# GpSimd's work outside the mixers moves to VectorE, and a tile's seven products run through three PSUM banks

## The chip, the cores and the metric

The kernel runs on one core of a Trainium2 chip. The metric is device time in microseconds (us). Three runs of the kernel before took 2840.35, 2843.02 and 2845.91 us; the median is 2843.02 us. A core has five engines that the profile names PE (TensorE, matmuls; its weight loads are PEld), DVE (VectorE), ACT (ScalarE), POOL (GpSimd) and SP (SyncE, which issues the loads). Each runs its own list of instructions in order and waits by semaphores for the others.

## The reference

Two layers of a hybrid backbone work on 512 latent tokens and 256 context tokens of width 1024. Each layer has a feed-forward part, a mixer (attention and others) and a second feed-forward part. The change touches the feed-forward parts and the vectors that modulate their inputs:

```python
def rms_norm(x, g):
    x32 = x.astype(jnp.float32)
    y = x32 * lax.rsqrt(jnp.mean(x32 * x32, axis=-1, keepdims=True) + EPS)
    return (y * g.astype(jnp.float32)).astype(x.dtype)

def modulate(h, shift, scale):
    return h * (1 + scale) + shift

def swiglu(h, w_gu, w_down):
    gate, up = jnp.split(h @ w_gu, 2, axis=-1)
    return (jax.nn.silu(gate) * up) @ w_down

def macaron_ffn(x, g, shift, scale, gate, w_gu, w_down):
    h = modulate(rms_norm(x, g), shift, scale)
    return x + 0.5 * gate * swiglu(h, w_gu, w_down)
```

Shift, scale and gate are products of a 1024 by 9216 matrix per layer with silu(c) for the latent tokens (vector 0 in the kernel) and with silu(c_ctx) for the context tokens (vector 1). The inner width of the feed-forward part is 2816, that is 22 tiles of 128.

## The kernel before

The activations stay in SBUF, features on partitions, tokens along the free axis. Every fp32 operand of a matmul is split in two parts: ACT casts the high part (`fill`, L324), DVE subtracts it from the source for the low part (L325), and each product is three matmuls (`mm3`, L303 to L305).

There are four feed-forward sub-layers. The text calls them FFN00, FFN01, FFN10 and FFN11 (layer, first or second). The first three work on 768 tokens, FFN11 on the 512 latent tokens. FFN00 runs to about 600 us of the profiled execution, FFN01 from about 1160 to 1640, FFN10 from about 1765 to 2200, FFN11 from about 2490 to the end; the mixers lie between.

In a feed-forward sub-layer the first three tiles (in FFN00 five) are plain products. The other tiles, 17 in FFN00 and 19 in each other sub-layer, are made by `gu_w`. It treats gate and up as a 2 by 2 block product and takes Winograd's seven block products in place of eight. Each of the seven is 12 matmuls (4 k tiles, three matmuls each) on half of the tokens: 384 columns, in FFN11 256. For that, sums of weight blocks are needed in each tile (POOL, L516, L517, L519, L522) and sums of input blocks once per sub-layer (`combos`: T1 and T2 on DVE, T3 and part of T4 on POOL, L486 to L488, L508, L509; cast and low part L481, L482). The seven products go to five PSUM banks. ACT copies two of them out (L541, L544), DVE adds the others in SBUF (L547 to L560), and the result is split (`finish`, L414, L415). After two to four tiles, a chunk, `down` multiplies them by the second matrix and DVE adds the result to the residual (L316).

FFN00 and FFN01 also carry jobs: `mod_jobs` works out the modulation vectors of later sub-layers from rows of weights, 128 rows by 512 features in a job. For vector 0 DVE multiplies and sums in one instruction (L153; a short one reads the sum out). For vector 1 POOL multiplies (L149) and ACT sums (L150). At the start of the program (`start_up`) the same is done with rows of 1024 for the first norm, tile by tile, between the first products, and POOL makes the low part of one of three weight tiles (L325). POOL also adds up the squares of all later norms (L239).

The order on each engine is set by a scheduler that works with modelled costs. `issue_after` fixes an instruction's turn behind another: products stand behind the last product (`pe_last`), jobs behind the last DVE step of a tile (`dve_last`), and the vector 1 multiply behind the last of the combos on POOL (`pool_last`). Raw weights have two buffers (`wraw`), split weight blocks six slots while there are jobs and eight otherwise, rows of the jobs two (`NWM`).

Of the kernel before, what the change touches and what calls it, by code (L numbers as in the profile page):

```python
# [15 lines left out]
ALU = mybir.AluOpType  # L16
# [37 lines left out]
def hybrid_backbone_kernel(ctx: ExitStack, tc: tile.TileContext, A: dict, out: bass.AP):  # L54
# [9 lines left out]
    def opened(name, **kw):  # L64
        """a pool that is open from here until its second part is called"""
        es = ExitStack()
        return es.enter_context(tc.tile_pool(name=name, bufs=1, reuse_waits="tile", **kw)), es.close

    # PSUM: four banks, and four more that are single or in pairs as the phase wants them
# [20 lines left out]
    # ---------------------------------------------------------------- constants  # L90
# [13 lines left out]
    def load_constants(pool, l, shape):  # L104
        """per-head gains (those of the queries with the scores' factor, negated), head selectors and their transposes"""
# [14 lines left out]
    # ---------------------------------------------------------------- work that is emitted between groups of products  # L120
    pending = []
    down_last, act_last, pool_last = [], [], []
# [13 lines left out]
    # ---------------------------------------------------------------- adaLN vectors  # L136
    def load_silc(tiles, d0, n):
        """silu(c) and silu(c_ctx), n elements from d0, on every partition"""
        for v, t in enumerate(tiles):
            nc.sync.dma_start(t, A["cb"][:, v, d0:d0 + n])  # L140
            ACT.activation(t, t, AF.Silu)
        return tiles

    def mod_row(w, junk, silc, vecs, outs, behind=()):
        """products of 128 rows of weights with silc, an element of the vector per partition"""
        for v in vecs:
            if v == 1:
                with issue_after(pool_last):
                    POOL.tensor_tensor(w, w, silc[v], op=ALU.mult)  # L149
                ACT.activation(w, w, AF.Copy, accum_out=outs[v])  # L150
                continue
            with issue_after(behind):
                V.tensor_tensor_reduce(junk, w, silc[v], 1.0, 0.0, ALU.mult, ALU.add, outs[v])  # L153
# [16 lines left out]
    def mod_jobs(items):  # L170
        """items: (layer, sub, kind, vecs); a job takes 128 elements' products with a half of the features"""
# [23 lines left out]
    # ---------------------------------------------------------------- root mean square, inverse  # L195
# [4 lines left out]
    def rsqrt_sqrt(y, v, pool, shape, tag):  # L200
        """y = v ** -0.5; y and v: [p, n]: root, reciprocal and a Newton step"""
# [8 lines left out]
    def rsqrt_newton(y, v, pool, shape, tag):  # L210
        """the same, v normal and above 0, without the root: a first guess by exponent, then three Newton steps"""
# [7 lines left out]
    class Norm:  # L219
        """RMSNorm and modulation of columns [c0, c0+n) of x into hh, hl"""  # L220

        def __init__(self, c0, n, l, s, eng=POOL, room=None, tail=0):
            self.tail = tail
            self.c0, self.n, self.l, self.s, self.eng = c0, n, l, s, eng
# [3 lines left out]
        def add(self, kt):  # L228
# [4 lines left out]
            else:  # L233
# [5 lines left out]
                self.eng.tensor_tensor(self.acc[:, :self.n], self.acc[:, :self.n], sq[:, :self.n], op=ALU.add)  # L239

        def sums(self):
# [9 lines left out]
            (rsqrt_newton if self.eng is V else rsqrt_sqrt)(y[:, :nt], ms[:, :nt], sm, [P, nt], "rt")  # L251
# [29 lines left out]
    # ---------------------------------------------------------------- weight blocks, split in two float32r parts  # L281
    def wsplit(pool, r, bufs, tag="w", eng=V):
        """[128, n] -> two float32r parts, n at most 1024"""
# [7 lines left out]
    def wload(src, n=2048, parts=2):  # L291
        """one load of two blocks"""
# [4 lines left out]
    def by_k(w, k=KT):  # L297
        """split block [128, k * c] -> one (high, low) pair per k tile"""
# [8 lines left out]
    def issue_after(ins):  # L307
        """what is traced inside takes its turn on the engine behind ins"""
# [9 lines left out]
    # ---------------------------------------------------------------- half-step SwiGLU  # L318
    def fill(w, src, eng=V, behind=()):
        """a float32 block -> its two float32r parts"""  # L320
# [9 lines left out]
    def lead_ffn(fi):  # L330
        """the weights of the first three tiles, a part at a time; then where they are, and how to let go of them"""
# [10 lines left out]
    def lead_mixer(src, name):  # L342
        """the first blocks of an input projection, likewise"""
# [15 lines left out]
    def ffn(l, f, with_ctx, jobs=(), next_sub=None, opening=False, lead_in=None, lead_out=None):  # L359
        """Gate and up products of a tile are a 2 by 2 block product (gate / up, halves of the features,  # L360
        halves of the tokens). The first tiles take it as it stands, while the norms and the sums of blocks
        are being finished; the others take Winograd's seven block products."""
# [10 lines left out]
        with tc.tile_pool(name=f"ffn{fi}", bufs=1, reuse_waits="tile") as fp:  # L373
# [10 lines left out]
            def lead_slots():  # L384
                """[128, 512] pairs for the weights of the first three tiles, a pair per two k tiles"""
# [20 lines left out]
            def lead_k(w):  # L406
                """per k tile: gate and up"""
# [9 lines left out]
            def activate(act, c0, g, u):  # L417
                """of one stream's gate and up"""
# [10 lines left out]
            def gate_up(n):  # L429
                """places for a gate and an up product of n columns"""  # L430
# [22 lines left out]
            def lead(ws, each=None):  # L453
                """first tiles, k outermost, one stream after the other, while the norms are being finished"""
# [20 lines left out]
            def combos():  # L475
                """sums of blocks of the input: T1, T2, T3 and -T4"""
# [17 lines left out]
                for k in range(4):  # L494
# [5 lines left out]
                    sums(POOL, b, b22, b12)  # L500
                    done(2, k, b)
                for k in range(4):
# [5 lines left out]
                    POOL.tensor_tensor(a, b21[0], b, op=ALU.subtract)  # L508
                    pool_last[:] = [POOL.tensor_tensor(a, a, b21[1], op=ALU.add)]  # L509
                    dve_last[:] = [done(3, k, a)]  # L510

            def gu_w(ft):
# [3 lines left out]
                POOL.tensor_tensor(f3, a11, a21, op=ALU.subtract)  # L516
                POOL.tensor_tensor(a21, a21, a22, op=ALU.add)  # L517
                s1 = put(a21)
                POOL.tensor_tensor(a11, a21, a11, op=ALU.subtract)  # L519
                s2 = put(a11)  # L520
                w12 = put(a12)
                POOL.tensor_tensor(a12, a12, a11, op=ALU.subtract)  # L522
                s4 = put(a12)
                s3 = put(f3)
# [12 lines left out]
                oa, oc, ob, od, oe = (bank()[:, :nh] for _ in range(5))  # L537
                sg = sg_tile()
                product(oa, w11, hh[:, TOP, H1], hl[:, TOP, H1])
                x1 = tmp("t2")  # L540
                ACT.copy(x1, oa)  # L541
                product(oc, s1, *tblk[0])
                x5 = tmp("t2")
                ACT.copy(x5, oc)  # L544
                product(ob, s2, *tblk[1])
                u2 = tmp("nacc")
                dve_last[:] = [V.tensor_tensor(u2, ob, x1, op=ALU.add)]  # L547
                product(oa, w12, hh[:, BOT, H1], hl[:, BOT, H1], first=False)
                ACT.activation(sg[:, H1], oa, AF.Silu)
# [3 lines left out]
                product(od, s3, *tblk[2])  # L553
                dve_last[:] = [V.tensor_tensor(u2, od, u2, op=ALU.add)]
                V.tensor_tensor(x5, x5, u2, op=ALU.add)
# [3 lines left out]
                product(oe, w22, *tblk[3])  # L559
                V.tensor_tensor(u2, oe, u2, op=ALU.add)  # L560
                V.tensor_tensor(sg[:, H1], sg[:, H1], u2, op=ALU.mult)
# [91 lines left out]
    def start_up(tiles, slots, lead_k, fill, lead):  # L653
        """loads, first adaLN vectors, first norm and first tiles of the first sub-layer, k by k"""
# [6 lines left out]
        nl = Norm(*LAT, 0, 0, V)  # L661
        nctx = Norm(*CT, 0, 0, V)
# [868 lines left out]
```

## Time and profile before

| | |
|---|---|
| median of 3 runs | 2843.02 us |
| span of the profiled execution | 2841.2 us |
| time around the span, to the median | 1.8 us |
| PE busy | 2648.6 us (93%) |
| DVE busy | 2188.0 us (77%) |
| ACT busy | 1213.8 us (43%) |
| POOL busy | 978.1 us (34%), 677 instructions |
| chain that ended last | PE 62%, DVE 18%, ACT 4%, POOL 2% |

The profile's page gives busy time and the granted clock of TensorE as shares of full speed; a clock of 1.00 is 2.4 GHz throughout, and a lower one is a mean over stretches at 2.4 and at 1.2 GHz. Busy time of an engine counts overlapping instructions once, so the durations in a list of instructions add up to somewhat more. Where a row ends in square brackets, the engine stood idle for that many us before the instruction, and the name behind the arrow is what ended the wait.

### The profile page before, as it was taken

How to read it: one execution, taken by the hardware profiler on the slowest of the kernel's cores; microseconds unless marked ns; L12 is line 12 of the kernel's file. 1: busy time of each engine (PE TensorE's matmuls, PEld its weight loads, DVE VectorE, ACT ScalarE, POOL GpSimd, SP SyncE). 2: the span in 40 equal slices, each digit the busy share in tenths (PEclk: the TensorE clock that was granted, in tenths of full speed). 3: DMA queues.
4: the chain of work that ended last, by engine and by line, in shares of the span. 5: the costliest groups of instructions: out<-in, count | busy, mean ns of one | idle time of the engine just before them, and what ended most of it. 6: DMA issues, size and time to landing. Idle time of an engine off the chain costs nothing.

```text
span 2841.2 us, 42081 instructions
## 1 busy us (share of the span) xinstructions
PE 2648.6 (93%) x15826; PEld 2393.1 (84%) x15826; DVE 2188.0 (77%) x3820; ACT 1213.8 (43%) x2512; POOL 978.1 (34%) x677
## 2 busy tenths in 40 slices
PE   3699999999999999899999988999999989999999
PEld 2589888987977788799899877999998767988988
DVE  8979889986466844998899877777777577577877
ACT  5334444444344542344444443333334455444443
POOL 4555545542121111555455323222212010143432
PEclk9899999999999999999999999999999999999999
DMA  6323333333111241133333321333323200303232
GB/s 236 106 75 117 123 110 123 112 114 117 63 55 48 67 158 38 49 123 113 121 112 108 99 83 53 107 104 108 115 97 104 81 31 1 119 35 108 93 108 90
DMA packets 81172, 271.69 MB, mean 96 GB/s; under 512 B 11002, under 2 KB 15518, under 8 KB 66248
## 3 DMA queue, kind: packets, MB, share of 16 engines
q1 hardware_dynamic: 80408, 268.76, 27.7%
q8 instruction: 124, 2.03, 0.3%
q14 instruction: 80, 0.66, 0.1%
q0 software_dynamic: 560, 0.24, 0.0%
HBM read 262.35 MB, written 5.24 MB: 94 GB/s over the span
## 4 chain that ended last, share of the span: by engine, by line
PE 62%; DVE 18%; ACT 4%; issue 3%; DMA 3%; POOL 2%; SPq 0%; DVEq 0%; ACTq 0%; POOLq 0%
PE ps L303 9%; PE ps L304 9%; PE ps L305 9%; PE pb L303 7%; PE pb L304 7%; PE pb L305 7%; DVE wl L325 5%; DVE junk L153 2%; PE pp L303 2%; PE pp L304 2%; PE pp L305 2%; PE ps L767 2%; ACT wh L324 2%; DVE xn L316 1%; DMA wm<-in_wmod 1%
## 5 line engine op out<-in xcount | busy, mean ns | idle before, releaser
L324 ACT CAST wh<-wr 128x512 fp32r<-128x512 f32 (+1 forms) x672 | 385.9, 590 | 571.6 <-PE pb L304 177.3
L325 DVE TENSOR_TENSOR wl<-wr,wh 128x512 fp32r<-128x512 f32 (+1 forms) x672 | 554.4, 837 | 93.7 <-ACT wh L324 88.8
L149 POOL TENSOR_TENSOR wm<-wm,silc 128x512 f32<-128x512 f32 x176 | 266.5, 1514 | 297.6 <-DVE mod L153 100.9
L303 PE MATMUL ps<-hh,wh 128*128 128x384 f32 (+2 forms) x728 | 252.1, 347 | 24.0 <-ACT u L541 18.9
L305 PE MATMUL ps<-hh,wl 128*128 128x384 f32 (+2 forms) x728 | 250.6, 344 | 2.2 <-DVE wl L325 1.2
L304 PE MATMUL ps<-hl,wh 128*128 128x384 f32 (+2 forms) x728 | 250.4, 344 | 0.0
L153 DVE CUSTOM_DVE_ANT_0 junk<-wm,silc 128x512 bf16<-128x512 f32 x240 | 225.2, 938 | 25.2 <-DMA wm<-in_wmod 20.1
L516 POOL TENSOR_TENSOR s<-wr 128x512 f32<-128x512 f32 x74 | 112.1, 1515 | 378.1 <-DMA wr<-in_wgs 245.8
L303 PE MATMUL pb<-hh,wh 128*128 128x384 f32 (+2 forms) x632 | 210.3, 333 | 29.6 <-ACT u L541 18.3
L304 PE MATMUL pb<-hl,wh 128*128 128x384 f32 (+2 forms) x632 | 209.4, 332 | 26.5 <-DVE hl L269 26.5
L303 PE MATMUL ps<-ah,wh 128*128 128x512 f32 (+1 forms) x640 | 218.9, 348 | 4.5 <-DVE u L560 3.7
L304 PE MATMUL ps<-al,wh 128*128 128x512 f32 (+1 forms) x640 | 220.7, 345 | 0.4 <-DVE al L415 0.4
L305 PE MATMUL ps<-ah,wl 128*128 128x512 f32 (+1 forms) x640 | 219.8, 344 | 0.0
L305 PE MATMUL pb<-hh,wl 128*128 128x384 f32 (+2 forms) x632 | 208.4, 330 | 0.2 <-DVE wl L325 0.2
L303 PE MATMUL pb<-tt,wh 128*128 128x384 f32 (+2 forms) x600 | 195.7, 326 | 13.5 <-ACT tt L481 13.5
L303 PE MATMUL pb<-ah,wh 128*128 128x512 f32 (+1 forms) x576 | 197.9, 354 | 7.6 <-DVE u L560 3.8
L304 PE MATMUL pb<-al,wh 128*128 128x512 f32 (+1 forms) x576 | 202.3, 351 | 2.5 <-DVE al L415 1.4
L304 PE MATMUL pb<-tt,wh 128*128 128x384 f32 (+2 forms) x600 | 196.4, 327 | 6.6 <-DVE tt L482 6.6
L305 PE MATMUL pb<-ah,wl 128*128 128x512 f32 (+1 forms) x576 | 200.8, 349 | 0.0
L305 PE MATMUL ps<-tt,wl 128*128 128x384 f32 (+1 forms) x600 | 195.6, 326 | 3.2 <-DVE wl L325 3.2
L303 PE MATMUL ps<-tt,wh 128*128 128x384 f32 (+1 forms) x600 | 195.3, 326 | 3.5 <-ACT wh L324 3.5
L305 PE MATMUL pb<-tt,wl 128*128 128x384 f32 (+2 forms) x600 | 195.8, 326 | 0.7 <-DVE wl L325 0.7
(373 smaller groups left out, 7379.1 us busy)
## 6 DMA issues: line engine op xcount, KB each, us to landing
wr<-in_wgs SPq DMA_DIRECT2D x76, 1024.0 KB
wm<-in_wmod SPq DMA_DIRECT2D x240, 256.0 KB
wr<-in_wdn SPq DMA_DIRECT2D x44, 768.0 KB
wr<-in_wdn SPq DMA_DIRECT2D x18, 512.0 KB
wr<-in_wgl SPq DMA_DIRECT2D x9, 1024.0 KB
wr<-in_wmod SPq DMA_DIRECT2D x16, 512.0 KB
wr<-in_wqk_ab SPq DMA_DIRECT2D x5, 1024.0 KB
bias<-in_bias_ab SPq DMA_DIRECT2D x12, 384.0 KB
```

Of the source, the lines that this page charges most:

```text
L149: POOL.tensor_tensor(w, w, silc[v], op=ALU.mult)
L153: V.tensor_tensor_reduce(junk, w, silc[v], 1.0, 0.0, ALU.mult, ALU.add, outs[v])
L303: PE.matmul(o, wh, rh, start=start, stop=False, skip_group_check=again)
L304: PE.matmul(o, wh, rl, start=False, stop=False, skip_group_check=again)
L305: return PE.matmul(o, wl, rh, start=False, stop=stop, skip_group_check=again)
L316: return V.scalar_tensor_tensor(xs, ps_ap, hgt[:, vec_index(c0), l * 3 + s, dt:dt + 1], xs, ALU.mult, ALU.add)
L324: ACT.copy(h[:, :n], src)
L325: eng.tensor_tensor(lo[:, :n], src, h[:, :n], op=ALU.subtract)
L516: POOL.tensor_tensor(f3, a11, a21, op=ALU.subtract)
L767: PE.transpose(out=o[:, c * P:(c + 1) * P], in_=p[:, c * P:(c + 1) * P], identity=ident)
```

## The change

All of POOL's work outside the mixers becomes DVE's: the four sums of weight blocks per tile, T3 and T4 of the input sums, the sums of squares, the low part of the third start-up tile, and vector 1 of the modulation, which now is the same single DVE instruction as vector 0; the sum on ACT (L150) goes. `Norm` has a flag for the way of its root in place of an engine; which norm takes which root is as before.

The seven products of a tile run in another order through three banks. Bank `ox` takes w11, s2, s3 and w22 in turn and adds them up; ACT copies it out after the first three of these (x1, u2, u3), and DVE multiplies with the bank itself at the end. `oc` takes s1, which ACT copies (x5), and s4 on top of it. `oa` takes w12, which moves from fourth to sixth place. Between a product into `ox` and the next one into it stands one other product, and one between s1 and s4. In the kernel before two stood between the copied bank's products (w11 and w12 in `oa`, s1 and s4 in `oc`). ACT's copies of a tile go from two to four, DVE's steps on the products from seven to five, and silu of the first half reads SBUF behind a DVE sum in place of PSUM.

```diff
         for v in vecs:
-            if v == 1:
-                with issue_after(pool_last):
-                    POOL.tensor_tensor(w, w, silc[v], op=ALU.mult)
-                ACT.activation(w, w, AF.Copy, accum_out=outs[v])
-                continue
             with issue_after(behind):
                 V.tensor_tensor_reduce(junk, w, silc[v], 1.0, 0.0, ALU.mult, ALU.add, outs[v])
...
-                self.eng.tensor_tensor(self.acc[:, :self.n], self.acc[:, :self.n], sq[:, :self.n], op=ALU.add)
+                V.tensor_tensor(self.acc[:, :self.n], self.acc[:, :self.n], sq[:, :self.n], op=ALU.add)
...
-                    sums(POOL, b, b22, b12)
+                    sums(V, b, b22, b12)
...
-                    POOL.tensor_tensor(a, b21[0], b, op=ALU.subtract)
-                    pool_last[:] = [POOL.tensor_tensor(a, a, b21[1], op=ALU.add)]
+                    V.tensor_tensor(a, b21[0], b, op=ALU.subtract)
+                    V.tensor_tensor(a, a, b21[1], op=ALU.add)
...
-                POOL.tensor_tensor(f3, a11, a21, op=ALU.subtract)
-                POOL.tensor_tensor(a21, a21, a22, op=ALU.add)
+                V.tensor_tensor(f3, a11, a21, op=ALU.subtract)
+                V.tensor_tensor(a21, a21, a22, op=ALU.add)
                 s1 = put(a21)
-                POOL.tensor_tensor(a11, a21, a11, op=ALU.subtract)
+                V.tensor_tensor(a11, a21, a11, op=ALU.subtract)
                 s2 = put(a11)
-                w12 = put(a12)
-                POOL.tensor_tensor(a12, a12, a11, op=ALU.subtract)
-                s4 = put(a12)
+                V.tensor_tensor(a11, a12, a11, op=ALU.subtract)
+                s4 = put(a11)
                 s3 = put(f3)
+                w12 = put(a12)
                 w22 = put(a22)
...
-                oa, oc, ob, od, oe = (bank()[:, :nh] for _ in range(5))
+                ox, oc, oa = (bank()[:, :nh] for _ in range(3))
...
-                product(oa, w11, hh[:, TOP, H1], hl[:, TOP, H1])
-                x1 = tmp("t2")
-                ACT.copy(x1, oa)
+                product(ox, w11, hh[:, TOP, H1], hl[:, TOP, H1])
+                x1 = keep("t2", ox)
                 product(oc, s1, *tblk[0])
-                x5 = tmp("t2")
-                ACT.copy(x5, oc)
-                product(ob, s2, *tblk[1])
-                u2 = tmp("nacc")
-                dve_last[:] = [V.tensor_tensor(u2, ob, x1, op=ALU.add)]
-                product(oa, w12, hh[:, BOT, H1], hl[:, BOT, H1], first=False)
-                ACT.activation(sg[:, H1], oa, AF.Silu)
+                x5 = keep("t2", oc)
+                product(ox, s2, *tblk[1], first=False)
+                u2 = keep("nacc", ox)
                 product(oc, s4, hh[:, BOT, H2], hl[:, BOT, H2], first=False)
                 dve_last[:] = [V.tensor_tensor(sg[:, H2], oc, u2, op=ALU.add)]
                 ACT.activation(sg[:, H2], sg[:, H2], AF.Silu)
-                product(od, s3, *tblk[2])
-                dve_last[:] = [V.tensor_tensor(u2, od, u2, op=ALU.add)]
-                V.tensor_tensor(x5, x5, u2, op=ALU.add)
+                product(ox, s3, *tblk[2], first=False)
+                u3 = keep("nacc", ox)
+                product(oa, w12, hh[:, BOT, H1], hl[:, BOT, H1])
+                dve_last[:] = [V.tensor_tensor(sg[:, H1], oa, x1, op=ALU.add)]
+                ACT.activation(sg[:, H1], sg[:, H1], AF.Silu)
+                V.tensor_tensor(x5, x5, u3, op=ALU.add)
                 V.tensor_tensor(sg[:, H2], sg[:, H2], x5, op=ALU.mult)
                 act = act_tiles()
                 finish(act, sg, H2)
-                product(oe, w22, *tblk[3])
-                V.tensor_tensor(u2, oe, u2, op=ALU.add)
-                V.tensor_tensor(sg[:, H1], sg[:, H1], u2, op=ALU.mult)
+                product(ox, w22, *tblk[3], first=False)
+                V.tensor_tensor(sg[:, H1], sg[:, H1], ox, op=ALU.mult)
                 finish(act, sg, H1)
...
-                fill([a[:, (kt % 2) * 256:(kt % 2) * 256 + 256] for a in slots[i][kt // 2]], ws[i], POOL if i == 0 else V)
+                fill([a[:, (kt % 2) * 256:(kt % 2) * 256 + 256] for a in slots[i][kt // 2]], ws[i])
```

The lines of the changed kernel have numbers about five lower: L153 becomes L148, L324 and L325 become L319 and L320, the weight sums L511, L512, L514 and L516, the copies L538.

The scheduler places the moved work as follows. POOL in the middle of FFN00, before: the sums of one tile (L516 to L522, `s` is the buffer of s3) and between them multiplies of vector 1 (L149).

```order
L516 TENSOR_TENSOR s_3754<-wr 128x512
L149 TENSOR_TENSOR wm<-wm,silc 128x512
L517 TENSOR_TENSOR wr<-wr 128x512
L519 TENSOR_TENSOR wr<-wr 128x512
L149 TENSOR_TENSOR wm<-wm,silc 128x512 x2
L522 TENSOR_TENSOR wr<-wr 128x512
L149 TENSOR_TENSOR wm<-wm,silc 128x512 x2
```

DVE of the changed kernel in a tile of FFN00: the sums (L514, L516) stand between low parts (L320), sums of the modulation (L148, each with its short read) and the add out of PSUM (L548).

```order
L148 ISA junk,mpart<-wm,silc 128x512
L148 ISA mpart 128x1
L514 TENSOR_TENSOR wr<-wr 128x512
L320 TENSOR_TENSOR wl<-wr,wh 128x512
L148 ISA junk,mpart<-wm,silc 128x512
L148 ISA mpart 128x1
L548 TENSOR_TENSOR sg<-ps,u 128x384
L320 TENSOR_TENSOR wl<-wr,wh 128x512
L148 ISA junk,mpart<-wm,silc 128x512
L148 ISA mpart 128x1
L516 TENSOR_TENSOR wr<-wr 128x512
```

What stood in two lists that ran side by side now stands in one, in turn. ACT in a tile of FFN00, before: the copies out of PSUM (L541, L544) stand among casts of weights (L324), casts of the finished activations (L414) and sums of vector 1 (L150).

```order
L324 CAST wh<-s_5548 128x512
L414 CAST ah<-sg 128x384
L150 ACTIVATE wm,mpart<-wm 128x512
L324 CAST wh<-wr 128x512
L541 COPY u<-ps 128x384
L414 CAST ah<-sg 128x384
L324 CAST wh<-wr 128x512
L544 COPY u<-pb 128x384
L324 CAST wh<-wr 128x512 x2
L549 ACTIVATE sg<-ps 128x384
```

ACT of the changed kernel at such a place:

```order
L319 CAST wh<-wr 128x512
L409 CAST ah<-sg 128x384
L319 CAST wh<-wr 128x512
L538 COPY u<-ps 128x384
L409 CAST ah<-sg 128x384
L319 CAST wh<-wr 128x512
L538 COPY u<-pb 128x384
L319 CAST wh<-wr 128x512
L538 COPY u<-ps 128x384
L319 CAST wh<-wr 128x512
L549 ACTIVATE sg<-sg 128x384
```

The sums of vector 1 are gone, four copies (all L538) take the place of two, and the last cast of the tile before (L409) still stands between two of them. DVE at the start of the program, before: sums of squares (L239), then sums of the modulation (L153), their finish (L159, L161) and low parts (L325).

```order
L153 ISA tt,mod<-wr,tt 128x1024
L153 ISA mod 128x1
L159 TENSOR_TENSOR mod<-mod,bmod 128x1
L239 TENSOR_TENSOR nacc<-nacc,t_172 128x512
L161 SCALAR_TENSOR_TENSOR gsc<-mod,ng 128x1
L153 ISA tt,mod<-wr,tt 128x1024
L153 ISA mod 128x1
L325 TENSOR_TENSOR wl<-tt,wh 128x256
L159 TENSOR_TENSOR mod<-mod,bmod 128x1
L325 TENSOR_TENSOR tt<-tt 128x256
```

DVE of the changed kernel at the same place:

```order
L148 ISA tt,mod<-wr,tt 128x1024
L148 ISA mod 128x1
L148 ISA tt,mod<-wr,tt 128x1024
L148 ISA mod 128x1
L154 TENSOR_TENSOR mod<-mod,bmod 128x1
L234 TENSOR_TENSOR nacc<-nacc,t_170 128x512
L148 ISA tt,mod<-wr,tt 128x1024
L148 ISA mod 128x1
L156 SCALAR_TENSOR_TENSOR gsc<-mod,ng 128x1
L320 TENSOR_TENSOR wl<-tt,wh 128x256 x2
L320 TENSOR_TENSOR tt<-tt 128x256
```

The sums of vector 1 stand among those of vector 0, ahead of the norm's root; up to the norm's spread (L253) it is 15 sums of 1024 where it was 4.

## Rows read from the trace of the kernel before

**Rows 1.** The page's first line

```profile
span 2841.2 us, 42081 instructions
```

**Rows 2.** Stretches: length, busy PE, PEld, DVE, ACT, POOL; clock, DMA share, GB/s

```profile
14.20:128.00 113.80, 60.67 (x226) 46.23 (x227) 112.85 (x165) 49.10 (x101) 68.58 (x32) 0.87 0.48 169
150.00:594.00 444.00, 415.80 (x2274) 389.80 (x2272) 395.69 (x624) 195.00 (x444) 242.95 (x165) 0.96 0.34 115
1170.00:1591.00 421.00, 392.22 (x2175) 372.05 (x2174) 373.35 (x578) 185.72 (x416) 217.89 (x146) 0.98 0.33 112
```

**Rows 3.** The same, a chunk of three tiles in each of the four

```profile
400.16:479.60 79.44, 74.80 (x401) 70.55 (x400) 70.79 (x112) 36.40 (x82) 41.74 (x29) 0.94 0.36 120
1384.40:1457.70 73.30, 71.24 (x403) 67.40 (x402) 64.36 (x104) 33.60 (x75) 36.64 (x26) 1.00 0.36 119
1877.00:1946.80 69.80, 69.80 (x399) 66.73 (x398) 49.80 (x92) 24.94 (x47) 16.27 (x13) 1.00 0.32 106
2664.80:2711.80 47.00, 46.18 (x324) 43.24 (x323) 36.76 (x64) 20.49 (x47) 17.33 (x13) 1.00 0.28 99
```

**Rows 4.** DVE by line, shape in FFN00's chunk: count, busy us, mean ns, idle

```profile
L325 DVE TENSOR_TENSOR wl<-wr,wh 128x512 fp32r<-128x512 f32 x18 | 17.9, 1002 | 0.6 <-ACT wh L324 0.3
L153 DVE CUSTOM_DVE_ANT_0 junk<-wm,silc 128x512 bf16<-128x512 f32 x16 | 16.7, 1042 | 5.6 <-ACT silc L141 2.8 <-DMA wm<-in_wmod 2.8
L325 DVE TENSOR_TENSOR wl<-wr,wh 128x384 fp32r<-128x384 f32 x9 | 7.6, 843 | 0.4 <-ACT wh L324 0.2
...
L561 DVE TENSOR_TENSOR sg<-sg,u 128x384 f32<-128x384 f32 x3 | 3.8, 1272 | 0.0
```

**Rows 5.** Timeline of DVE in FFN00: start and duration in us

```profile
400.48 1.39 DVE L325 TENSOR_TENSOR wl<-wr,wh 128x384 fp32r<-128x384 f32 x1
...
406.55 0.55 DVE L325 TENSOR_TENSOR wl<-wr,wh 128x384 fp32r<-128x384 f32 x1
...
407.67 0.68 DVE L153 CUSTOM_DVE_ANT_0 junk<-wm,silc 128x512 bf16<-128x512 f32 x1
...
411.12 0.67 DVE L325 TENSOR_TENSOR wl<-wr,wh 128x512 fp32r<-128x512 f32 x1
411.72 0.68 DVE L153 CUSTOM_DVE_ANT_0 junk<-wm,silc 128x512 bf16<-128x512 f32 x1
```

**Rows 6.** Timeline of POOL, the same stretch

```profile
400.16 1.29 POOL L516 TENSOR_TENSOR s<-wr 128x512 f32<-128x512 f32 x1 [1.08 <-DMA wr<-in_wgs]
```

**Rows 7.** What PE waited for: us in total, times, longest

```profile
PE ps L303 <- ACT u L541: 18.9, 11, 3.1
PE pb L303 <- ACT u L541: 18.3, 9, 3.6
...
PE pb L303 <- ACT tt L481: 13.5, 2, 10.1
```

**Rows 8.** DVE by line and shape at the start (14.2 to 128 us)

```profile
L153 DVE CUSTOM_DVE_ANT_0 tt<-wr,tt 128x1024 bf16<-128x1024 f32 x16 | 20.8, 1301 | 0.0
L325 DVE TENSOR_TENSOR tt<-tt 128x256 fp32r<-128x256 f32 x12 | 16.5, 1385 | 0.0
L153 DVE CUSTOM_DVE_ANT_0 tt<-tt 128x1024 bf16<-128x1024 f32 x8 | 13.6, 1698 | 0.0
L269 DVE SCALAR_TENSOR_TENSOR hl<-t,mod,hh 128x512 fp32r<-128x512 f32 x8 | 13.3, 1665 | 0.7 <-ACT hh L268 0.7
L159 DVE TENSOR_TENSOR mod<-mod,bmod 128x1 f32<-128x1 f32 x16 | 10.0, 622 | 0.1
```

**Rows 9.** End of product w11 on PE and its copy on ACT, FFN00

```profile
359.40 0.34 PE L305 MATMUL ps<-hh,wl 128*128 128x384 f32 x1
...
366.59 0.47 ACT L541 COPY u<-ps 128x384 f32<-128x384 f32 x1
```

**Rows 10.** The same in FFN10

```profile
1831.42 0.34 PE L305 MATMUL ps<-hh,wl 128*128 128x384 f32 x1
...
1832.15 0.47 ACT L541 COPY u<-ps 128x384 f32<-128x384 f32 x1
```

More of the change, by code (lines that the diff above doesn't have):

```diff
@@ L121, in hybrid_backbone_kernel @@
     pending = []
-    down_last, act_last, pool_last = [], [], []
+    down_last, act_last = [], []
     def pump(n=1):
@@ L219, in hybrid_backbone_kernel, with __init__ @@
     class Norm:
-        def __init__(self, c0, n, l, s, eng=POOL, room=None, tail=0):
+        def __init__(self, c0, n, l, s, newton=False, room=None, tail=0):
             self.tail = tail
-            self.c0, self.n, self.l, self.s, self.eng = c0, n, l, s, eng
+            self.c0, self.n, self.l, self.s, self.newton = c0, n, l, s, newton
             self.room = room or (lambda: sm.tile([P, 512], F32, tag="t2", name="t2"))
@@ L250, in sums @@
             y = sm.tile([P, 4], F32, tag="ry", name="ry")
-            (rsqrt_newton if self.eng is V else rsqrt_sqrt)(y[:, :nt], ms[:, :nt], sm, [P, nt], "rt")
+            (rsqrt_newton if self.newton else rsqrt_sqrt)(y[:, :nt], ms[:, :nt], sm, [P, nt], "rt")
             self.dg = sm.tile([P, 512], F32, tag="nacc", name="dg", bufs=2)
@@ L515, in gu_w @@
                 f3 = s3_tile()
-                POOL.tensor_tensor(f3, a11, a21, op=ALU.subtract)
-                POOL.tensor_tensor(a21, a21, a22, op=ALU.add)
+                V.tensor_tensor(f3, a11, a21, op=ALU.subtract)
+                V.tensor_tensor(a21, a21, a22, op=ALU.add)
                 s1 = put(a21)
-                POOL.tensor_tensor(a11, a21, a11, op=ALU.subtract)
+                V.tensor_tensor(a11, a21, a11, op=ALU.subtract)
                 s2 = put(a11)
+                V.tensor_tensor(a11, a12, a11, op=ALU.subtract)
+                s4 = put(a11)
+                s3 = put(f3)
                 w12 = put(a12)
-                POOL.tensor_tensor(a12, a12, a11, op=ALU.subtract)
-                s4 = put(a12)
-                s3 = put(f3)
                 w22 = put(a22)
@@ L535, in tmp, with keep @@
                     return sm.tile([P, 512], F32, tag=tag, name="u", bufs=2)[:, :nh]
-                oa, oc, ob, od, oe = (bank()[:, :nh] for _ in range(5))
+                ox, oc, oa = (bank()[:, :nh] for _ in range(3))
                 sg = sg_tile()
-                product(oa, w11, hh[:, TOP, H1], hl[:, TOP, H1])
-                x1 = tmp("t2")
-                ACT.copy(x1, oa)
-                product(oc, s1, *tblk[0])
-                x5 = tmp("t2")
-                ACT.copy(x5, oc)
-                product(ob, s2, *tblk[1])
-                u2 = tmp("nacc")
-                dve_last[:] = [V.tensor_tensor(u2, ob, x1, op=ALU.add)]
-                product(oa, w12, hh[:, BOT, H1], hl[:, BOT, H1], first=False)
-                ACT.activation(sg[:, H1], oa, AF.Silu)
+                def keep(tag, o):
+                    t = tmp(tag)
+                    ACT.copy(t, o)
+                    return t
+                product(ox, w11, hh[:, TOP, H1], hl[:, TOP, H1])
+                x1 = keep("t2", ox)
+                product(oc, s1, *tblk[0])
+                x5 = keep("t2", oc)
+                product(ox, s2, *tblk[1], first=False)
+                u2 = keep("nacc", ox)
                 product(oc, s4, hh[:, BOT, H2], hl[:, BOT, H2], first=False)
@@ L660, in start_up @@
         nc.sync.dma_start(bmod, A["bmod"])
-        nl = Norm(*LAT, 0, 0, V)
-        nctx = Norm(*CT, 0, 0, V)
+        nl = Norm(*LAT, 0, 0, True)
+        nctx = Norm(*CT, 0, 0, True)
         def row(kind, kt, w):
```

## The prediction

> **What bounds the kernel now.** I read the table of stretches first, then the same table for single chunks, the list of DVE's instructions by line and shape, the timelines of DVE and POOL, PE's waits, and at last the two engines around a copy out of PSUM. The span is 2841.2 us [rows 1], and 1.8 us lie around it to the median of 2843.0; the sum below is made on the span.
>
> PE is busy for most of the span, but that is a mean over unlike stages. At the start (14.2 to 128 us) DVE is busy for 112.85 of 113.80 us and PE for 60.67: DVE bounds. In FFN00 (150 to 594) and FFN01 (1170 to 1591) PE has 415.80 of 444.00 and 392.22 of 421.00, DVE 395.69 and 373.35: both are near full and each waits for the other [rows 2]. The same work, a chunk of three tiles with its `down`, shows what PE needs: 69.80 us in FFN10, where PE is never idle and the granted clock is 1.00. In FFN00 it takes 79.44 with a clock of 0.94, in FFN01 73.30 [rows 3]. So 9.64 us per chunk can be won in FFN00, 3.50 in FFN01 and nothing in FFN10. FFN11 has 0.82 us of idle PE in its chunk.
>
> DVE's time in these chunks is partly not its own work. A low part of 384 columns takes 0.55 us alone and 1.39 us when POOL's L516 runs beside it from 400.16 to 401.45 [rows 5, 6]: DVE is held until POOL ends. Over FFN00's chunk the low parts of 512 columns have a mean of 1002 ns where the clean one took 0.67; L153 has 1042 where the clean one took 0.68; those of 384 have 843, L561 has 1272 [rows 4, 5]. The excess is 18 x 0.33 + 16 x 0.36 + 9 x 0.29 + 3 x 0.72 = 16.5 us, and four smaller kinds of the same view bring it to 21.0. The same count in FFN01's chunk gives 17.4.
>
> **The change part by part.** *DVE in FFN00's chunk.* Added: four sums per tile, 12 in a chunk, and 16 sums of vector 1. A 512-column step started at 411.12, the next at 411.72 [rows 5]: 0.60 us each, though its duration reads 0.67. The sum of vector 1 is the L153 form, 0.61 by the same measure. Removed: two steps on products per tile, 6 x 0.48 (0.55 less the same overlap). So 70.8 - 21.0 + 7.2 + 9.8 - 2.9 = 63.9 us of DVE in place of 70.8. With DVE at its present share (70.79 / 79.44 = 0.89) the chunk takes 71.7, 7.7 less; the stage is 444.00 / 79.44 = 5.6 chunks, so -43 us. With full durations in place of start-to-start times DVE has 66.9, the chunk 75.1, and the stage gains 24. PE's floor of 69.80 gives -54. I take -33, the middle of the first two, since two nearly full engines do not meet at either's floor.
>
> The Trainium skill ("VectorE: DVE Perf Modes", section The DRAIN you can't avoid) says that after an operation the next one doesn't start until the pipe is empty, which would make full durations the price and the gain 24. The rows say the opposite for this kernel: the next start lies 0.07 us ahead of the end [rows 5].
>
> *FFN01's chunk*: 64.4 - 17.4 + 7.2 + 13 x 0.61 - 2.9 = 59.2, at its share of 0.88 67.4, under PE's floor. So PE would bound: -3.5 x 5.7 = -20. I take -14, for idle that DVE does not cause.
>
> *FFN10 and FFN11.* There are no vector 1 jobs. Even with no lock-out taken off, DVE has 49.8 + 7.2 - 2.9 = 54.1 of 69.80, and 36.76 + 7.2 - 2.2 = 41.8 of 47.00 [rows 3]; PE hides it. 0, between -6 (FFN11's idle in some seven chunks) and +10, if DVE at 0.89 of FFN11's chunk begins to hold PE by 1.5 us in each.
>
> *The start.* DVE's held-up instructions: 12 low parts at 1385 ns (alone 0.41: 11.7), 16 L159 at 622 (0.15: 7.6), 8 L269 at 1665 (0.74: 7.4), 8 L153 at 1698 and 16 at 1301 (1.21: 3.9 and 1.4) [rows 8]; nine smaller kinds of that view bring 32.0 to 51.0. Added: 24 sums of 1024 at 1.30 = 31.2 and eight low parts at 0.41 = 3.3. So 112.9 - 51.0 + 34.5 = 96.4, that is -16.5 where DVE is the bound. Against it stand the 11 more sums of 1024 that the new order puts ahead of the first norm's spread: about 14 us of DVE less the locks that go there, so that the first product starts some 7 us later. DVE is never without work, so that shifts work rather than adding any, but the last tiles then wait on PE a little. I take -12, between 0 and -17.
>
> *Sums of the input.* PE waits 13.5 us for L481 behind them [rows 7], and other waits of this kind bring it to 20. T3 and T4 as three and two steps of about 0.5 us on DVE compete with T1 and T2 on one engine, but no POOL step of twice that length stands in the chain and none holds DVE. -8, between +5 and -20.
>
> *The three banks.* A copy out of `oa` is covered by two products before; a copy out of `ox` or `oc` by one, that is 12 matmuls of 384 columns, 2.1 us (w11 of rows 9 began at 357.47). The copy of w11 in FFN00 ended at 367.06, when w11 had ended at 359.74: 7.3 us later [rows 9]. In FFN10 it ended 0.9 us after [rows 10]. Even with two products of cover PE waited for these copies 20 times, 37.2 us in all [rows 7]. Halving the cover costs up to 2.1 us for a late copy. One per tile in the 36 tiles of FFN00 and FFN01 would be 76 us; none, if the copies come as early as in FFN10. What holds them is ACT's list: casts of weights that wait for POOL's sums, sums of vector 1 that wait for POOL, and casts that wait for DVE's last steps of the tile before. The first two go, the last stays, on a DVE with some room. Behind a waiting copy stand casts of the next weights, and PE waits for those. I take +20, between 0 and +76, nearer to the lower end because the row of FFN10 shows what an ACT without these waits does.
>
> The Trainium skill ("TensorE: Matmul & The Clock Gate", section A second HAM failure mode: psum-queue depth-cycling) tells of a kernel that cycles through PSUM banks, whose short PE idles between groups made the clock change back and forth. That speaks against more waits at banks. The chunk rows bear it out in part: 4.6 us idle goes with 0.94 in FFN00, but 2.1 us idle with 1.00 in FFN01 [rows 3]. If the short idles of the new scheme cost FFN01 what FFN00's cost it, 0.06 of 69.80 us for 5.7 chunks, that is +24; it belongs to the slower rival.
>
> *Loads.* POOL's first sum of a chunk waited 1.08 us for its weights [rows 6]. On DVE such a wait holds the low parts and PSUM steps queued behind it. 14 chunks of FFN00 and FFN01 at 0 to 1.1 us: +2, between 0 and +15.
>
> Sum: -33 - 14 + 0 - 12 - 8 + 20 + 2 = -45. The span becomes 2796, and with the 1.8 us around it 2798.
>
> **The rivals.** *PE becomes the bound in all four sub-layers.* The lock-out is gone and the clock stays at 1.00, the copies come in time: -54 - 20 - 17 - 20, that is 2732. For it: DVE's sum in FFN01 lies under PE's floor. Against: in FFN00 63.9 of 69.8 would be 0.92 of DVE, with copies and casts in series with it.
>
> *DVE stays the pace-setter.* The work moved to it waits in order, for loads and for ACT's casts, and its share falls to 63.9 / 79.44 = 0.80 in FFN00 (59.2 / 73.30 = 0.81 in FFN01). Then these stages do not get shorter, the start and the input sums give 20, the copies take as much: 2843, within 6 us of the time now. For it: all waits that POOL took (1.08 us for a load) now hold DVE. Against: DVE was kept at 0.89 with more in its way.
>
> *Slower: the copies hold PE.* If ACT's copy out of `ox` still ends more than 2.1 us after its product in the typical tile of FFN00 and FFN01, each chain w11, s2, s3, w22 is paced by PE, ACT, PE, and DVE's saving is worth nothing. The price: three quarters of 76 us, less the 20 of the start and the input sums: 2880, at the worst 2899. For it: 7.3 us in rows 9, and that the copies double while the last cast of the tile before still stands among them. Against: rows 10, and that ACT is busy for 36.40 of 79.44 us only.
>
> **How the numbers follow.** Forecast 0.60, its own range 2750 to 2830. PE bound 0.14, 2732. Pace-setter 0.10, 2843. Slower 0.16, 2880. The range reaches from 2735, just above the floor, to 2855, which leaves out most of the slower rival and the end of the faster one. 0.2% (5.7 us) is about what a measurement of this kernel can tell from no change. Faster: 0.60 + 0.14 and a part of the pace-setter, 0.77. Same: 0.07. Slower: 0.16.
>
> **What would show it.** Right: the 512-column low parts of DVE in FFN00 have a mean near 0.68 us; DVE's busy time in a chunk falls to 64 to 67 us; the chunk takes 72 to 75; DVE's work at the start ends before 118 us though the first product comes later than before; PE's waits for the copies stay under 60 us in all. Wrong: PE's waits for L538 above 100 us with a clock under 0.94 in FFN00 (the slower rival), or DVE idle for more than 15 us per chunk of FFN00 behind loads and casts (pace-setter).

## The result and the profile after

The changed kernel takes 2735.39 us (median of 4 runs, 2733.09 to 2738.62) against 2844.28 us for the kernel before in the same comparison: ratio 0.9619, 95% interval 0.9606 to 0.9633, faster by 3.8%. The forecast was 2798. The time lies 0.4 us above the lower end of its range (2735 to 2855) and next to the rival in which PE becomes the bound (2732, with a chance of 0.14), so that it is the rival that came and not the forecast.

The stretches of the three-tile chunks of [rows 3], found again by the first sum of a chunk on DVE. The columns are those of [rows 2]: length, busy PE, PEld, DVE, ACT, POOL; clock, DMA share, GB/s.

```profile
347.51:418.36 70.85, 70.85 (x404) 67.62 (x403) 62.90 (x149) 28.71 (x55) 0.00 (x0) 1.00 0.41 136
1291.58:1359.88 68.30, 68.30 (x391) 65.39 (x390) 59.27 (x136) 28.68 (x55) 0.00 (x0) 1.00 0.37 124
1769.66:1839.27 69.61, 69.61 (x399) 66.59 (x398) 51.40 (x99) 27.47 (x53) 0.00 (x0) 1.00 0.31 107
2554.80:2601.19 46.39, 46.39 (x325) 43.58 (x325) 37.38 (x71) 23.87 (x54) 0.00 (x0) 1.00 0.30 103
```

PE is never idle in any of them and holds 2.4 GHz throughout. DVE has 62.90 us in FFN00 and 59.27 in FFN01, where the sums of the prediction gave 63.9 and 59.2. DVE is busy for 0.89 of FFN00's chunk, the share that it had before, and PE waits for nothing.

The same chunk in FFN00, DVE by line and shape (count, busy us, mean ns, idle), against [rows 4]:

```profile
L148 DVE CUSTOM_DVE_ANT_0 junk<-wm,silc 128x512 bf16<-128x512 f32 x32 | 22.0, 687 | 3.2 <-ACT silc L141 1.7 <-DMA wm<-in_wmod 1.5
L320 DVE TENSOR_TENSOR wl<-wr,wh 128x512 fp32r<-128x512 f32 x18 | 12.4, 687 | 0.0
...
L320 DVE TENSOR_TENSOR wl<-wr,wh 128x384 fp32r<-128x384 f32 x8 | 4.4, 554 | 0.7 <-ACT wh L319 0.7
```

The means are those of an instruction alone: 687 ns in place of 1002 and 1042.

Both kernels run the same 15826 matmuls, so the stretches of [rows 2] can be found again by the count of matmuls. FFN00's takes 397.2 us (444.4 before), FFN01's 398.5 (421.0 before); the start's ends at 100.5 us in place of 128.1:

```profile
122.60:519.80 397.20, 397.20 (x2275) 376.42 (x2274) 364.72 (x834) 155.62 (x303) 0.00 (x0) 1.00 0.38 126
1087.90:1486.40 398.50, 383.51 (x2174) 367.51 (x2174) 344.75 (x772) 159.78 (x308) 0.00 (x0) 0.98 0.36 117
```

Of the 47 us in FFN00, 28 were idle time of PE. The other 19 came off its busy time, 415.80 to 397.20 us for the same matmuls, as the granted clock rose from 0.96 to 1.00.

End of w11 on PE and its copy on ACT, in the first tile whose products PE runs in FFN00's chunk, against [rows 9]:

```profile
372.49 0.34 PE L300 MATMUL ps<-hh,wl 128*128 128x384 f32 x1
```

```profile
373.27 0.48 ACT L538 COPY u<-ps 128x384 f32<-128x384 f32 x1
```

The copy ends at 373.75, 0.92 us after the product; the next product into that bank began at 374.79, so one product covers it. The median of FFN00's 17 Winograd tiles is 0.9 us, and it was 4.8 before; the 7.3 us of [rows 9] belong to one of the later copies. What PE still waited for in the whole run (total, times, longest):

```profile
PE pb L298 <- ACT u L538: 28.7, 3, 15.0
...
PE ps L254 <- DVE dg L248: 22.5, 2, 19.2
...
PE ps L298 <- ACT u L538: 5.2, 2, 4.0
```

Two of the five waits for a copy stand at the first Winograd tile of FFN01 and of FFN10 (15.0 and 12.3 us), right behind the sums of the input; the other three are in FFN11. Before, PE waited 9.6 and 10.6 us in these two tiles (L481 and L482). In FFN00 and in the rest of FFN01 and FFN10 PE waits for no copy.

The stages, cut at the spread of the norms on PE (us, worked out from the starts of these matmuls in each trace). A stage begins with the first spread for the context tokens and ends with the first of the next norm; what lies between the spreads of one norm is left out. The last column is the median of the runs:

| | start | FFN00 | mixer | FFN01 | FFN10 | mixer | FFN11 | run |
|---|---|---|---|---|---|---|---|---|
| before | 107.5 | 551.0 | 404.7 | 558.8 | 523.9 | 252.1 | 354.9 | 2843.0 |
| after | 84.9 | 499.7 | 399.6 | 530.8 | 523.5 | 255.7 | 346.4 | 2735.4 |
| e1 moves | 85.5 | 505.7 | 402.8 | 534.0 | 525.9 | 257.1 | 344.7 | 2743.4 |
| e2 banks | 108.9 | 547.8 | 405.4 | 558.6 | 524.7 | 254.1 | 356.0 | 2849.4 |
| e3 mod only | 86.2 | 507.2 | 402.0 | 536.9 | 524.4 | 257.4 | 353.8 | 2761.3 |
| e4 sums only | 108.3 | 530.5 | 402.5 | 534.4 | 525.3 | 251.7 | 347.1 | 2792.2 |
| e11 free read | 85.1 | 581.3 | 404.7 | 589.2 | 531.7 | 258.0 | 368.8 | 2912.7 |
| e7 direct 4 | 85.4 | 499.2 | 401.7 | 519.8 | 509.9 | 257.4 | 342.1 | 2709.6 |

Of the 109 us the start gave 23, FFN00 51, FFN01 28, FFN11 8.5; FFN10, where PE had been full, gave nothing.

### The profile page after: what moved, and what is told of

Its sections match the earlier page's. It is cut to its first block, busy times and chain, and to the rows that moved or that the text cites. A ratio compares the mean times of both kernels' runs of the same rounds, so it can differ in the third digit from the quotient of the medians.

```text
span 2731.3 us, 41348 instructions
## 1 busy us (share of the span) xinstructions
PE 2605.7 (95%) x15826; PEld 2367.9 (87%) x15826; DVE 2112.2 (77%) x4506; ACT 1147.6 (42%) x2260; POOL 66.0 (2%) x43
## 4 chain that ended last, share of the span: by engine, by line
PE 86%; DVE 9%; ACT 2%; DMA 1%; issue 1%; SPq 0%; DVEq 0%; ACTq 0%
PE ps L298 13%; PE ps L299 13%; PE ps L300 12%; PE pb L299 11%; PE pb L298 11%; PE pb L300 11%; PE pp L298 2%; PE pp L299 2%; PE pp L300 2%; PE ps L766 2%; DVE xn L311 1%; PE ps L1077 1%; PE ps L1012 1%; PE ps L1331 1%; DVE wl L320 1%
## 5 line engine op out<-in xcount | busy, mean ns | idle before, releaser
L319 ACT CAST wh<-wr 128x512 fp32r<-128x512 f32 (+1 forms) x672 | 391.6, 592 | 754.8 <-PE pb L299 259.8
L320 DVE TENSOR_TENSOR wl<-wr,wh 128x512 fp32r<-128x512 f32 (+1 forms) x672 | 434.4, 651 | 107.8 <-ACT wh L319 105.0
L148 DVE CUSTOM_DVE_ANT_0 junk<-wm,silc 128x512 bf16<-128x512 f32 x416 | 284.4, 684 | 7.2 <-ACT silc L141 4.6
L298 PE MATMUL ps<-hh,wh 128*128 128x384 f32 (+2 forms) x728 | 245.4, 338 | 2.0 <-ACT wh L282 1.4
L300 PE MATMUL ps<-hh,wl 128*128 128x384 f32 (+2 forms) x728 | 244.2, 336 | 1.0 <-DVE wl L283 1.0
L299 PE MATMUL ps<-hl,wh 128*128 128x384 f32 (+2 forms) x728 | 244.3, 336 | 0.0
L298 PE MATMUL pb<-hh,wh 128*128 128x384 f32 (+2 forms) x632 | 204.0, 323 | 5.1 <-ACT hh L263 4.7
L299 PE MATMUL pb<-hl,wh 128*128 128x384 f32 (+2 forms) x632 | 203.3, 322 | 3.0 <-DVE hl L264 2.9
L298 PE MATMUL ps<-tt,wh 128*128 128x384 f32 (+1 forms) x600 | 194.0, 324 | 5.2 <-ACT u L538 5.2
L299 PE MATMUL ps<-tt,wh 128*128 128x384 f32 (+1 forms) x600 | 194.5, 324 | 0.0
L311 DVE SCALAR_TENSOR_TENSOR xn<-ps,hgt,xn 128x512 f32<-128x512 f32 (+1 forms) x184 | 117.8, 645 | 41.6 <-PE ps L300 40.7
```

Of the source, the lines that this page charges most:

```text
L298: PE.matmul(o, wh, rh, start=start, stop=False, skip_group_check=again)
L299: PE.matmul(o, wh, rl, start=False, stop=False, skip_group_check=again)
L300: return PE.matmul(o, wl, rh, start=False, stop=stop, skip_group_check=again)
L311: return V.scalar_tensor_tensor(xs, ps_ap, hgt[:, vec_index(c0), l * 3 + s, dt:dt + 1], xs, ALU.mult, ALU.add)
L319: ACT.copy(h[:, :n], src)
L320: eng.tensor_tensor(lo[:, :n], src, h[:, :n], op=ALU.subtract)
```

## The experiments

**e1: the moves alone.** Start from the changed kernel; `gu_w` takes the old products.

```diff
-                ox, oc, oa = (bank()[:, :nh] for _ in range(3))
+                oa, oc, ob, od, oe = (bank()[:, :nh] for _ in range(5))
...
-                V.tensor_tensor(a11, a12, a11, op=ALU.subtract)
+                V.tensor_tensor(a12, a12, a11, op=ALU.subtract)
```

> All of POOL's work outside the mixers on DVE, the seven products in their old order through five banks. Theory A (the gain is the moved work: DVE is no longer held by POOL, and ACT no longer waits for POOL): 2735 to 2765 us, most of the 109 us of the whole change, and PE's waits for the copies out of PSUM, 37 us before, fall under 10. Theory B (the gain needs the three banks, since they take two steps per tile off DVE and give ACT copies that nothing but PE releases): 2790 to 2830 us.

2743.36 us, ratio 0.9651 (0.9633 to 0.9669). Theory A holds: 100 of the 109 us. The copies are on time (median 0.92 us after w11 in FFN00), and PE waits for none of them. DVE's total busy time fell, from 2188.0 us to 2168.6, although all of POOL's work outside the mixers was added to it:

```profile
PE 2617.1 (95%) x15826; PEld 2371.7 (86%) x15826; DVE 2168.6 (79%) x4654; ACT 1080.9 (39%) x2112; POOL 66.5 (2%) x43
```

**e2: the banks alone**, POOL keeps its work.

```diff
-                oa, oc, ob, od, oe = (bank()[:, :nh] for _ in range(5))
+                ox, oc, oa = (bank()[:, :nh] for _ in range(3))
...
-                POOL.tensor_tensor(a12, a12, a11, op=ALU.subtract)
+                POOL.tensor_tensor(a11, a12, a11, op=ALU.subtract)
```

> The new product order through three banks, with all of POOL's work left on POOL. Theory A: with ACT's list still waiting for POOL, copies stay 4 to 5 us late in FFN00 and FFN01 while one product covers only 2.1, so it is slower than before: 2860 to 2900 us. Theory B: two steps less per tile on DVE and no loss at the banks: 2800 to 2830 us.

2849.39 us, ratio 1.0022 (1.0012 to 1.0031). Slower, as A says, but by 6 us and not by 17 to 57. PE's waits for the copies did rise, from 41.8 us (37.2 for w11 [rows 7] and 4.6 for s1, L544) to 83.5:

```profile
PE pb L303 <- ACT u L543: 43.8, 20, 12.9
PE ps L303 <- ACT u L543: 39.7, 22, 9.4
```

The half cover thus does what the prediction feared while POOL runs, but PE's idle time in all rose only from 192.6 to 203.5 us: most of the new waits replace others. DVE's total busy time is 2112.6 us in place of 2188.0. The copies were not 4 to 5 us late either: in FFN00 the median fell from 4.8 to 1.0 us for w11 and from 4.1 to 2.7 for s1, with POOL's work still on POOL. A PE that waits at the bank gives ACT time to catch up, which may be why; no run separates it. Neither theory had both sides. On top of the moves the banks give 8 us (2743.4 to 2735.4).

**e3: vector 1 alone; e4: the sums of weight blocks alone.**

```diff
-            if v == 1:
-                with issue_after(pool_last):
-                    POOL.tensor_tensor(w, w, silc[v], op=ALU.mult)
-                ACT.activation(w, w, AF.Copy, accum_out=outs[v])
-                continue
```

> Only vector 1 of the modulation moves to DVE, and its sum leaves ACT. Theory A: the part of the lock-out that L149 causes goes (some 60% of POOL's time in FFN00, all of it at the start): 2780 to 2805 us. Theory B: DVE takes 134 us more in the sub-layers with jobs and gains little: 2835 to 2860 us.

```diff
-                POOL.tensor_tensor(f3, a11, a21, op=ALU.subtract)
+                V.tensor_tensor(f3, a11, a21, op=ALU.subtract)
```

(and the three others likewise)

> Only the four sums of weight blocks per tile move to DVE; vector 1 stays on POOL and ACT. Theory A: the lock-out of the sums goes but that of L149 stays, and ACT still waits for POOL's L149: 2800 to 2830 us. Theory B: 2840 to 2870 us, since DVE gets four more steps per tile without the two that the banks save.

e3: 2761.25, ratio 0.9712 (0.9693 to 0.9731). e4: 2792.17, ratio 0.9826 (0.9804 to 0.9847). They lie 19 and 8 us below A's ranges and far below B's. Their gains, 82 and 51 us, add to more than the 100 of e1: each alone already gives nearly all of FFN01's gain (536.9 and 534.4 us, both together 534.0). The start's 22 us belong to vector 1 (21 in e3, none in e4), FFN11's gain to the sums of weight blocks (8 us in e4, 1 in e3).

**e5, e6: POOL's work without its results.** The changed kernel, with unread POOL instructions of 512 columns (e6: 256): four per tile, and one per row of vector 1.

```diff
+                POOL.tensor_tensor(scr, a12[:, :512], a22[:, :512], op=ALU.subtract)   # four times
...
+                        if 1 in vecs:
+                            POOL.tensor_tensor(state["scr"], w[:, :512], state["silc"][1][:, :512], op=ALU.mult)
```

> The changed kernel, plus POOL instructions whose results nobody reads: four differences of two weight blocks of 512 columns per tile and one multiply of 512 per row of vector 1 in FFN00 and FFN01, as many and as long as POOL had there before. No engine but the buffers of the loads waits for them. Theory A1 (POOL's mere running beside DVE holds DVE): back up by most of what the moves gave in the sub-layers, 2790 to 2830 us, and DVE's low parts of 512 columns in FFN00 again above 900 ns. Theory A2 (what cost time was that ACT and DVE waited for POOL's results): within 10 us of 2735.

> The same POOL instructions with half the columns (256). A1: about half of the loss of the full ones, 2760 to 2785 us. A2: 2735 within 10 us.

e5: 3022.14 us, 287 more than the changed kernel (ratio to before 1.0637, 1.0615 to 1.0658). e6: 2822.55, 87 more (0.9926, 0.9903 to 0.9948). In FFN00 (150 to 560 us) DVE's low parts of 512 columns have a mean of 1013 and 821 ns. Both losses are larger than A1 said; that DVE now carries the moved work as well is a likely reason, but not shown. These instructions also hold the load buffers until POOL is done; in e5 SP's queue waited 25 us for that.

**e8: POOL only writes**, tied to the same loads and buffers: copies of one column, and two memsets in place of each sum or multiply.

```diff
+                POOL.tensor_copy(scr[:, :1], a12[:, :1])
+                POOL.memset(scr, 0.0)
+                POOL.memset(scr[:, :640], 0.0)
...
```

> As the full unread POOL work, but POOL only writes: in place of each difference or multiply a pair of memsets (960 and 640 columns) between copies of single columns, which tie it to the same loads and hold the same buffers. Theory R (POOL's reading of SBUF is what holds DVE): 2735 within 15 us, DVE's low parts of 512 columns at 0.69 us. Theory W (any POOL instruction beside DVE holds it, or the held load buffers cost the time): 2900 us or more, as with the reading ones.

2791.59 us, ratio 0.9816 (0.9799 to 0.9833): 56 above the changed kernel, so the time expected of R was missed, though DVE's means stayed at 686 and 684 ns with POOL busy for 1053.0 us. The loads paid: SP's queue waited for POOL, 337 us in all.

```profile
SPq L295 <- POOL scr L541: 89.6, 16, 9.1
```

**e10, e11: a buffer held only for one tying copy**; after it POOL works on a scratch tile alone.

```diff
+                POOL.tensor_copy(scr[:, :1], a12[:, :1])
+                for _ in range(4):
+                    POOL.memset(scr, 0.0)                                     # e10
+                    POOL.tensor_tensor(scr, scr, scr, op=ALU.subtract)        # e11
...
```

> Unread POOL work again, now without holding any load buffer for long: one copy of a single column ties it to the load, then POOL works on a scratch tile alone. Here it only writes: one memset of 960 columns (0.90 us) in place of each sum or multiply. If reading is what holds DVE and the 56 us of the earlier write-only version came from held load buffers: 2735 to 2745 us. If a busy POOL costs time in another way: 2765 us or more.

> The same, but POOL reads the scratch tile twice and writes it (a difference of 512 columns, about 1.5 us). No load buffer is held and nobody waits for POOL, so what is lost is DVE being held alone: 2850 to 2960 us, with DVE's low parts of 512 columns at 0.85 to 0.9 us as a mean over the run. If the time in the full version came from the held buffers: below 2790 us.

e10: 2752.27 us (0.9688, 0.9666 to 0.9710), 17 above the changed kernel, 7 more than expected. None of the 17 lie in the stretches found by the count of matmuls (397.3 and 398.6 us, for 397.2 and 398.5); 10 come up from the end of FFN00 into the mixer (480 to 640 us), and their cause is open. e11: 2912.73 us (1.0245, 1.0209 to 1.0282), 177 above it, as expected; its two stretches take 461.7 and 452.3 us. DVE's low parts of 512 columns and the modulation's sums over the whole run in the changed kernel, e10 and e11:

```profile
L320 DVE TENSOR_TENSOR wl<-wr,wh 128x512 fp32r<-128x512 f32 x496 | 338.5, 686 | 64.4 <-ACT wh L319 61.9
L148 DVE CUSTOM_DVE_ANT_0 junk<-wm,silc 128x512 bf16<-128x512 f32 x416 | 284.4, 684 | 7.2 <-ACT silc L141 4.6 <-DMA wm<-in_wmod 2.3
```

```profile
L324 DVE TENSOR_TENSOR wl<-wr,wh 128x512 fp32r<-128x512 f32 x496 | 338.1, 686 | 68.3 <-ACT wh L323 66.2
L148 DVE CUSTOM_DVE_ANT_0 junk<-wm,silc 128x512 bf16<-128x512 f32 x416 | 284.4, 684 | 3.9 <-ACT silc L141 1.9 <-DMA wm<-in_wmod 1.4
...
L529 POOL MEMSET scr<- 128x960 f32 x296 | 267.1, 902 | 17.2
```

```profile
L324 DVE TENSOR_TENSOR wl<-wr,wh 128x512 fp32r<-128x512 f32 x496 | 397.1, 807 | 44.7 <-ACT wh L323 43.7
L148 DVE CUSTOM_DVE_ANT_0 junk<-wm,silc 128x512 bf16<-128x512 f32 x416 | 349.9, 841 | 4.3 <-DMA wm<-in_wmod 1.9 <-ACT silc L141 1.7
...
L530 POOL TENSOR_TENSOR scr<-scr 128x512 f32<-128x512 f32 x296 | 382.5, 1292 | 23.3
```

A POOL that only writes leaves DVE's mean durations as they were. One that reads two operands lengthens them (807 ns, where 850 to 900 had been expected; 924 in FFN00 from 150 to 560 us), and DVE's total busy time rises from 2112.2 to 2383.6 us. POOL's work is longer in e11 than in e10 (609 us against 426), but e8's was longer still and left the durations alone. PE's waits for copies come back with it. No compute engine waits for this work of POOL, and SP's queue as little as in e10 (24.2 us in e11 and 24.4 in e10 for the next tile's weights):

```profile
PE pb L302 <- ACT u L548: 86.7, 37, 20.9
PE ps L302 <- ACT u L548: 49.2, 33, 4.6
```

So a held DVE is enough to bring late copies back; ACT's waits for POOL are not needed for them. The way is probably through ACT's list: its casts of weight sums (`wh<-wr`) wait 299 us for DVE, and 128 in the changed kernel. How much ACT's waits for POOL and its sums of vector 1 cost beside that in the kernel before was not separated.

**e7, e9: one more plain tile ahead of the input sums.**

```diff
-NDIRECT = (5, 3, 3, 3)
+NDIRECT = (5, 4, 4, 4)
```

In e9 FFN00 has one less besides: (4, 4, 4, 4).

> The changed kernel, in which FFN01, FFN10 and FFN11 take one more tile as plain products (eight in place of seven) ahead of the sums of the input. In the changed kernel PE waits 15.0, 12.3 and 5.5 us at the first product that needs these sums. If DVE has them ready behind a tile of plain products: -15 - 12 - 5 us, +2.1, +2.1 and +1.4 us for the eighth products: 2705 to 2720 us. If DVE is merely later with them, since it is the weights' low parts that it does first: 2735 to 2745 us.

> The version with one more tile of plain products in FFN01, FFN10 and FFN11, and in FFN00 one less (four in place of five). If FFN00's sums of the input are ready behind one tile: 2.1 us less than that version, about 2707 us. If they are not, PE waits for them as it did in FFN01: 2715 to 2725 us.

e7: 2709.63 us, ratio to before 0.9538 (0.9523 to 0.9553), the fastest of all, and in the range expected if DVE has the sums ready; FFN01 and FFN10 lose 11 and 14 us, FFN11 4. All waits for copies are 3.3 and 1.5 us in the whole run now; the one at FFN01's first Winograd tile is 1.6 in place of 15.0, and FFN10's is gone.

e9: 2713.63 (0.9546, 0.9532 to 0.9561), 4 us more than e7 and between the two expectations: FFN00 took 505.3 us in place of 499.2, with a wait of 8.2 us at its first Winograd tile.

## Why the prediction was right or wrong

The forecast was -45 us and the kernel gained 109. The mechanism was right, and two steps of the sum failed: the price of the three banks, and the choice of a value between the bounds in FFN00 and FFN01. e1 divides the miss. Without the banks the terms add up to -65, and the moves alone gave -100; for the banks the sum had +20, and they gave -8 on top of the moves.

- *DVE is held by POOL; the moves shorten its chunk.* Right, and sized right: 62.9 and 59.3 us for 63.9 and 59.2. e10 and e11 show the cause. With full durations it would have been 66.9 in FFN00; the measured 62.9 speaks for start-to-start times. The first sentences on the DRAIN in the Trainium skill ("VectorE: DVE Perf Modes", section The DRAIN you can't avoid) would give full durations, and its last one says that a next operation that is not held starts earlier, which the prediction left out; the rows agree with the last one, 0.60 us from start to start at a duration of 0.67 [rows 5].
- *FFN00: -33, "two nearly full engines do not meet at either's floor".* Wrong step. PE did come to its floor: the chunk fell to 70.85 us with PE at 100% and DVE still at 0.89, and the whole stretch is full as well. Counted by the same matmuls the stretch lost 47 us, which is thus what the floor was worth; the -54 came from scaling up one chunk. DVE's old share as a limit gave -43, close to that, though nothing shows that this share was a limit: it stayed at 0.89 while PE's waits went. The error was the -24 that full durations gave, and the -33 in the middle.
- *FFN01: -14.* The same error: -22.5 by the same matmuls, past the floor's -20, although the wait of 15.0 us at the first Winograd tile lies in the stretch; the idle kept back "that DVE does not cause" was not there.
- *The three banks: +20.* Wrong step, and wrong in sign: -8 on top of the moves. The prediction read the lateness of 7.3 us in [rows 9] as a property of ACT's list that would partly stay. It went with POOL's work: in e1 the copies end 0.9 us after their products, as in [rows 10], and e11 shows that a held DVE is enough to make them late again. With POOL still running the price is 6 us net (e2).
- *The start: -12.* Undersized: -22.6 up to the spread for the context tokens, -27.6 to the end of the stretch. The first spread did come later (PE's wait for dg is 19.2 us in place of 14.9), as said, but DVE's own work set the end, and it is busy for 86.2 us up to there in place of 96.4. Six of the added sums come behind that point (7.3 us), and the sum took 1.30 us for each where it had put a clean one at 1.21 (measured 1.22). The 11 sums put ahead were work that had to be done anyway, and nothing was to be deducted for them.
- *The input sums: -8.* Wrong in sign: PE waits 15.0 and 12.3 us at the first Winograd tiles of FFN01 and FFN10, where it waited 9.6 and 10.6 before. T3 and T4 on DVE did not bring the sums earlier. e7 shows what lay there.
- *FFN10 and FFN11: 0.* Right for FFN10 (523.9 to 523.5). FFN11 gave 8.5, more than the 6 at most; e4 has 7.8 of it from the sums of weight blocks alone.
- *Loads, +2; the clock.* DVE waited 1.3 us for weights in FFN00's chunk, but PE did not wait in these chunks, and the granted clock was 1.00 in all four. The Trainium skill ("TensorE: Matmul & The Clock Gate", section A second HAM failure mode: psum-queue depth-cycling) tells of short idles between groups. In these chunks they did not arise. In e11, where PE waited 70 times for copies, the granted clock was 0.96 in both stretches of FFN00 and FFN01 (1.00 and 0.98 in the changed kernel), which agrees with it as far as a mean clock can.

Of the prediction's own signs, the low parts' mean (687 ns), the start and PE's waits for copies (33.9 us) came as written; the chunk's 70.85 us and DVE's 62.9 lie below what it named. The terms were set in the middle of their bounds one by one. The moves, one cause, took those of FFN00, FFN01, the banks and the start past the values set; the input sums alone went the other way. The rival's 2732 is nearly the time, but in part by luck: its -20 for the input sums did not come, and the start and FFN11, where it had -17 and nothing, made up for that.

## What to carry to other kernels

Where VectorE's time per instruction is well above that of the same instruction alone, look for GpSimd beside it: a slower engine's help can cost the faster one as much as the work itself (e1: 2188.0 us of VectorE with the help and 2168.6 without). And before pricing a thinner cover for a copy, ask what makes the copy late now, and whether the change takes just that away. Two engines at 0.9 of a stage each are no proof that neither can come to its floor.

## What the runs showed of the hardware

A GpSimd instruction that reads two SBUF operands holds VectorE's instructions with two operands in SBUF until it ends (0.55 to 1.39 us for 384 columns [rows 5, 6]); a memset of 960 columns, 0.90 us long, does not lengthen them (a mean of 686 ns with it and without). VectorE's adds to the residual, with one tensor in PSUM and one in SBUF, are not lengthened even in e11: 743 ns for 512 columns (L315) against 746 in the changed kernel (L311). Long GpSimd instructions with a single operand to read were not tested. Some 736 us of unread two-operand work on GpSimd (e5) cost VectorE 403 us of busy time (2112.2 to 2514.8). The Trainium skill ("SBUF — State Buffer", section Who interferes with whom) says that a VectorE instruction with two SBUF inputs contends with a GpSimd instruction that reads SBUF and not with one that only writes; e10 and e11 agree, with 686 against 807 ns.
